# Expert gates added into a cleared DRAM array by 4-byte indirect DMAs in place of one-hot products

## The chip, the cores and the metric

The kernel runs on one core of a Trainium2 chip. The metric is the device time of one execution in microseconds (us); the median of three runs of the kernel before is 4406.32 us. A core has TensorE (PE in the rows, its weight loads PEld), VectorE (DVE), ScalarE (ACT), GpSimd (POOL) and SyncE (SP). SP and POOL issue DMAs, which run on 16 DMA engines.

## The reference

One inference step of a two-layer hybrid model over two streams: 128 prompt tokens and 512 sample tokens, 1024 channels each. Layer 0 mixes tokens by retention and a short convolution, layer 1 by gated DeltaNet and a long convolution. After each mixer comes a channel mixer (PEER): each token picks 16 of 16,384 experts for each of 8 heads. The part that the change touches:

```python
def peer_ffn(h, wq, keys, u_tab, v_tab):
    ...
    s1, i1 = lax.top_k(s[:, :, 0], TOPK)
    s2, i2 = lax.top_k(s[:, :, 1], TOPK)
    cand_s = (s1[..., :, None] + s2[..., None, :]).reshape(T, H_P, TOPK * TOPK)
    cand_i = (i1[..., :, None] * N_KEYS + i2[..., None, :]).reshape(T, H_P, TOPK * TOPK)
    top_s, sel = lax.top_k(cand_s, TOPK)
    eidx = jnp.take_along_axis(cand_i, sel, axis=-1)
    gates = jax.nn.softmax(top_s.astype(jnp.float32), axis=-1).astype(h.dtype)
    ...
        act = jax.nn.gelu(jnp.einsum('td,tkd->tk', xt, u_tab[et]))
        return jnp.einsum('tk,tkd->td', gt * act, v_tab[et])
```

So the result for a token is the sum over its 128 chosen experts (i1, i2) of gate x gelu(u . h) x v. A head chooses an expert at most once, but two heads may choose the same one; their gates then add up.

## The kernel before

**Streams and tiles.** The sample stream has four tiles of 128 tokens. Its first three go through the dense way: activations of all 16,384 experts on TensorE, weighted by a gate matrix that is zero where an expert isn't chosen. The fourth tile (`gt`), and the prompt's one tile, go the sparse way (`peer_gather`): for each of 128 places a row of u, later a row of v, is fetched for each token by an indirect DMA from POOL (`row<-u,eid`, `row<-v,eid`), and VectorE multiplies or adds (`gacc`).

**Stages of `peer_dense`,** once per layer.
- Acts stage. `acts` takes a block of 128 experts (one i1) at a time: load `ur`, split it into two parts `uh` and `ul` (`u_split`; the subtraction for `ul` goes to VectorE and POOL in turn), 24 products into `A`, gelu, store to DRAM (`wd`). It runs in the background, at a rate of blocks per us of foreground (RA, RG, RH, RM). The foreground makes, in order, the lists of experts (`peer_topk`, one tile after the other, with eight multiplications `eq` on POOL each), the gate matrix (`gate_matrix`), and, in layer 0 alone, the prompt's mixer of layer 1 (`mid`).
- `gate_matrix`. For each token two one-hot rows are made on VectorE or ScalarE (`o1`, with the gate in place of the one, and `o2`), a product `G` puts the gates of a token at (i2, i1), ScalarE evicts four tokens at a time into `gst`, and SP stores 1 MB at a time to DRAM (`gd<-gst`).
- Dense stage. For each block of 128 experts `load` brings `vr`, the activations and, for eight blocks at a time, the gates (`gt<-gd`); `stage` splits v (`vh`, `vl`, on VectorE for even blocks and POOL for odd ones), multiplies the activations by the gates (`w<-w,gt`) and splits the product (`wh`, `wl`); 18 products go into six accumulators (`dacc`). Some blocks of layer 1 are "fused": their activations are computed here and not in the acts stage. F1 sets how many (62 of 128 in effect).

In both stages a few steps of the last tile's `peer_gather` go in with each block (rates G0, G1, SP, SF).

**Order of work.** In the acts stage POOL keeps the order of the program; the other engines, and SP throughout, are ordered by the scheduler that builds the kernel. In the dense stage POOL, VectorE and ScalarE keep the program's order.

**The start.** `modulation` makes the 48 columns of scale and shift of layer 0 from 512 KB pieces (`w<-ada_c`, `w<-ada_k`) that SP loads; the first norm of layer 0 needs the first 16 of them.

## Time and profile before

| | |
|---|---|
| runs | 4391.36, 4406.32, 4421.05 us; median 4406.32 |
| profiled execution | span 4406.5 us (first to last instruction) |
| PE, DVE, POOL, ACT busy | 88%, 83%, 55%, 34% of the span |
| mean granted TensorE clock | 0.938 of full speed |
| DMA | 1158.45 MB, 263 GB/s over the span |

Layer 0's acts stage runs from about 780 to 1740 us (lists until 1098, gate matrix until 1409, then the prompt's mixer), its dense stage to 2340. Layer 1's acts stage runs from 3142 to 3580 (lists until 3372, then the gate matrix), its dense stage to 4390. Busy time of engines that work at the same time doesn't add up; what matters in a stage is which engine or transfer the others wait for.

### The profile page before, as it was taken

How to read it: one execution, taken by the hardware profiler on the slowest of the kernel's cores; microseconds unless marked ns; L12 is line 12 of the kernel's file. 1: busy time of each engine (PE TensorE's matmuls, PEld its weight loads, DVE VectorE, ACT ScalarE, POOL GpSimd, SP SyncE). 2: the span in 40 equal slices, each digit the busy share in tenths (PEclk: the TensorE clock that was granted, in tenths of full speed). 3: DMA queues.
4: the chain of work that ended last, by engine and by line, in shares of the span. 5: the costliest groups of instructions: out<-in, count | busy, mean ns of one | idle time of the engine just before them, and what ended most of it. 6: DMA issues, size and time to landing. Idle time of an engine off the chain costs nothing.

```text
span 4406.5 us, 56677 instructions
## 1 busy us (share of the span) xinstructions
PE 3868.7 (88%) x19422; PEld 3206.9 (73%) x19422; DVE 3677.7 (83%) x6843; ACT 1498.3 (34%) x2828; POOL 2411.8 (55%) x1520
## 2 busy tenths in 40 slices
PE   6797858899999998899998987887589989999997
PEld 4453547899998987677775456756579978888886
DVE  6568889998998656988887997659989978888888
ACT  2110131122774442233332253532224743333333
POOL 0126673686143754766655777425265247776664
PEclk9998878789999999999999989899899999999999
DMA  7548886886688788899987967237256699989994
GB/s 284 172 157 328 288 305 232 310 316 228 237 301 304 246 284 307 269 320 319 320 304 278 339 225 236 65 120 253 72 202 224 256 321 327 326 311 319 322 318 171
DMA packets 437040, 1158.45 MB, mean 263 GB/s; under 512 B 39440, under 2 KB 188048, under 8 KB 430352
## 3 DMA queue, kind: packets, MB, share of 16 engines
q1 hardware_dynamic: 282064, 591.69, 38.5%
q0 software_dynamic: 154688, 563.15, 36.3%
q8 instruction: 152, 2.49, 0.2%
q14 instruction: 136, 1.11, 0.1%
HBM read 1060.71 MB, written 93.98 MB: 262 GB/s over the span
## 4 chain that ended last, share of the span: by engine, by line
PE 31%; DVE 16%; issue 10%; POOL 3%; ACT 2%; DMA 2%; SPq 0%; DVEq 0%; POOLq 0%; ACTq 0%
PE dacc L161 14%; PE A L161 10%; DVE row L1227 3%; DVE gacc L1237 3%; POOL row L1203 2%; PE po L161 2%; PE G L161 1%; DVE wl L1308 1%; ACT wh L1307 1%; DMA row<-v,eid 1%; DMA row<-u,eid 1%; PE pt L161 1%; DVE ul L1308 1%; DVE eq L1179 1%; DVE o L1299 1%
## 5 line engine op out<-in xcount | busy, mean ns | idle before, releaser
L161 PE MATMUL A<-hHL,uh 128*128 128x384 f32 x4096 | 1110.4, 351 | 25.9 <-ACT uh L1307 25.7
L1203 POOL DMA_INDIRECT row<-v,eid x512 | 672.9, 1314 | 491.3 <-DVE gacc L1237 195.7
L1227 DVE SCALAR_TENSOR_TENSOR row<-row,hn 128x1024 f32<-128x1024 f32 x512 | 701.3, 1385 | 153.5 <-DMA row<-u,eid 151.8
L1203 POOL DMA_INDIRECT row<-u,eid x512 | 688.0, 1344 | 249.9 <-DVE row L1227 110.3
L161 PEld LDWEIGHTS A<-hHL,uh 128*128 128x128 f32 x4096 | 767.9, 196 | 40.0 <-ACT uh L1307 28.4
L1237 DVE SCALAR_TENSOR_TENSOR gacc<-row,gel,gacc 128x1024 f32<-128x1024 f32 x508 | 744.6, 1466 | 55.3 <-DMA row<-v,eid 50.6
L161 PE MATMUL A<-hHL,ul 128*128 128x384 f32 x2048 | 721.0, 353 | 65.4 <-DVE ul L1308 59.8
L1308 POOL TENSOR_TENSOR ul<-ur,uh 128x1024 fp32r<-128x1024 f32 x128 | 334.1, 2610 | 504.0 <-ACT uh L1307 456.0
L161 PE MATMUL dacc<-vh,wh 128*128 128x512 f32 x1536 | 458.7, 397 | 77.2 <-ACT wh L1307 77.1
L1308 POOL TENSOR_TENSOR vl<-vr,vh 128x1024 fp32r<-128x1024 f32 x128 | 355.3, 2776 | 267.9 <-ACT vh L1307 146.3
L161 PE MATMUL dacc<-vl,wh 128*128 128x512 f32 x1536 | 474.9, 392 | 1.3 <-POOL vl L1308 1.3
L161 PE MATMUL dacc<-vh,wl 128*128 128x512 f32 x1536 | 457.9, 390 | 7.9 <-DVE wl L1308 7.9
L1307 ACT CAST wh<-w 128x384 fp32r<-128x384 f32 (+1 forms) x226 | 133.0, 589 | 963.6 <-DVE w L1451 422.0
L161 PEld LDWEIGHTS A<-hHL,ul 128*128 128x128 f32 x2048 | 400.8, 196 | 79.1 <-DVE ul L1308 67.2
L161 PE MATMUL pt<-hT,w 128*128 128x128 f32 (+1 forms) x1664 | 395.6, 395 | 22.9 <-DMA w<-wq 11.6
L1307 ACT CAST uh<-ur 128x1024 fp32r<-128x1024 f32 x256 | 267.7, 1046 | 422.5 <-PE A L161 288.6
L161 PEld LDWEIGHTS dacc<-vh,wh 128*128 128x128 f32 x1536 | 282.1, 189 | 161.2 <-ACT wh L1307 110.6
L161 PEld LDWEIGHTS pt<-hT,w 128*128 128x128 f32 x1664 | 246.4, 199 | 164.6 <-issue 143.8
L161 PEld LDWEIGHTS dacc<-vh,wl 128*128 128x128 f32 x1536 | 287.7, 188 | 73.3 <-DVE wl L1308 11.4
L161 PEld LDWEIGHTS dacc<-vl,wh 128*128 128x128 f32 x1536 | 288.4, 188 | 60.4 <-POOL vl L1308 2.6
L1307 ACT CAST vh<-vr 128x1024 fp32r<-128x1024 f32 x256 | 267.2, 1044 | 4.5 <-DMA vr<-v 4.4
L1451 DVE TENSOR_TENSOR w<-w,gt 128x384 f32<-128x384 f32 x194 | 243.8, 1257 | 3.7 <-DMA w<-wd 3.7
(373 smaller groups left out, 6160.3 us busy)
## 6 DMA issues: line engine op xcount, KB each, us to landing
ur<-ut SPq DMA_DIRECT2D x256, 512.0 KB, 4.6
vr<-v SPq DMA_DIRECT2D x256, 512.0 KB, 6.7
gd<-gst SPq DMA_DIRECT2D x48, 1024.0 KB, 5.7
gt<-gd SPq DMA_DIRECT2D x96, 512.0 KB, 7.8
wd<-w SPq DMA_DIRECT2D x194, 192.0 KB, 3.8
w<-wd SPq DMA_DIRECT2D x194, 192.0 KB, 6.4
w<-ada_k SPq DMA_DIRECT2D x56, 512.0 KB, 6.4
w<-wq SPq DMA_DIRECT2D x48, 512.0 KB, 5.3
```

The source lines that it names most:

```text
L161: self.nc.tensor.matmul(out, lhsT, rhs, start=start, stop=stop)
L1179: V.tensor_tensor(eq, sf[:, h, :].unsqueeze(2).to_broadcast([P, TOPK, NSLOT]), self.iota50.unsqueeze(1).to_broadcast([P, TOPK, NSLOT]), op ...
L1203: self.nc.gpsimd.indirect_dma_start(out=t, out_offset=None, in_=table, in_offset=bass.IndirectOffsetOnAxis(ap=idx, axis=0))
L1227: V.scalar_tensor_tensor(u, u, 1.0, hn, op0=OP.mult, op1=OP.mult, accum_out=act[:, k:k + 1])
L1237: V.scalar_tensor_tensor(gacc, v, t[:, k:k + 1], gacc, op0=OP.mult, op1=OP.add)
L1299: V.tensor_scalar(o1, self.iota128, cols[:, 0, t:t + 1], cols[:, 2, t:t + 1], op0=OP.is_equal, op1=OP.mult)
L1307: self.nc.scalar.copy(hi, src)
L1308: (eng or self.nc.vector).tensor_tensor(lo, src, hi.bitcast(F32), op=OP.subtract)
L1451: V.tensor_tensor(w.rearrange("p (b t) -> p b t", t=TB), w.rearrange("p (b t) -> p b t", t=TB), g[:, :, e % GQ, :], op=OP.mult)
```

## The change

Six DRAM arrays, one per layer and dense tile, 8 MB each, are cleared by 24 DMAs from a tile of zeros (`clear`). When a tile's list is there, `scatter` adds its gates into its array: one indirect DMA per column of the list, 128 tokens x 4 bytes, with an addition at the destination. Of each tile, the 16 columns of one head go out without waits between them; the next 16 wait until those have landed, as two heads may meet at one place. When two additions of the same tile follow each other, a small memset of `tick0` stands between them. The address, expert x 128 + token, comes out of `peer_topk`. The loads of the gates wait for the last 16 additions of their tile.

Along with it: the last tile's list is made last, not first; all `ul` splits of the acts stage go to VectorE; the background's additions go in at 4.5 or 5 per block; 39 blocks of layer 1 are fused in place of 62; the gates are loaded for four blocks at a time; and rates change.

```diff
-TB = 16
-GQ = 8
+GQ = 4
+GS0 = 4.5
+GS1 = 5
+ZW = 256
+ZN = 4
...
-GE = 56
+GE = 80
...
-RM = 0.7
+RM = 0.9
...
-F1 = 64
+F1 = 40
...
-P1 = 1.35
+P1 = 1.4
...
+    def clear(self, l, n):
+        nc = self.nc
+        self.gd[l] = [self.tc.dram_tile([P * P * P, 1], F32, name=self.nm("gd")) for _ in range(n)]
+        self.filled[l] = []
+        src = self.zero.unsqueeze(1).to_broadcast([P, P * P // ZW // ZN, ZW])
+        for g in self.gd[l]:
+            parts = g.rearrange("(p z a w) o -> z p a (w o)", p=P, z=ZN, w=ZW)
+            self.filled[l].append([])
+            for z in range(ZN):
+                self.filled[l][-1].append(nc.sync.dma_start(parts[z], src))
+                yield
...
+    def scatter(self, st, l, tiles):
+        nc = self.nc
+        at = {n: 0 for n in range(len(tiles))}
+        before, now = dict(enumerate(self.filled[l])), {n: [] for n in at}
+        last, turn = None, 0
+        while at:
+            ready = [n for n in at if tiles[n] in st.gate]
+            if not ready:
+                yield
+                continue
+            turn += 1
+            n = ready[turn % len(ready)]
+            if n == last:
+                nc.gpsimd.memset(self.tick0, 0.0)
+            last, c, it = n, at[n], tiles[n]
+            i = nc.gpsimd.indirect_dma_start(
+                out=self.gd[l][n], out_offset=bass.IndirectOffsetOnAxis(ap=st.eid[it][:, c:c + 1], axis=0),
+                in_=st.gate[it][:, c:c + 1], in_offset=None, compute_op=OP.add)
...
+            self.after(i, before[n])
+            now[n].append(i)
+            at[n] += 1
+            if at[n] % TOPK == 0:
+                before[n], now[n] = now[n], []
+            if at[n] == P:
+                del at[n]
+            yield
+        self.filled[l] = [before[n] for n in range(len(tiles))]
...
-            un = self.u_split(i + 1, ur.pop(i + 1), up) if i + 1 < len(es) else None
+            un = self.u_split(0, ur.pop(i + 1), up) if i + 1 < len(es) else None
...
+            put += (GS0, GS1)[l] if st.gate else 0
+            while put >= 1:
+                put -= 1
+                next(places, None)
...
+                    self.after(nc.sync.dma_start(gg[g][:, n], gd[n][:, g * GQ:(g + 1) * GQ, :]), self.filled[l][n])
...
+                for it in tiles:
+                    self.peer_topk(st, it, True)
                 self.peer_topk(st, gt)
-                for it in tiles:
-                    self.peer_topk(st, it)
...
-            with self.tc.tile_pool(name=self.nm("gp"), bufs=2, reuse_waits="tile") as self.gp:
-                self.gate_matrix(st, tiles, gd)
...
+            self.finish_bg()
+            for _ in places:
+                pass
             lp = self.tc.alloc_tile_pool(name=self.nm("loads"), bufs=1, side="right", reuse_waits="tile")
             for e in range(LA):
                 load(e)
-            self.finish_bg()
...
+                fill = K.clear(0, ss.nt - 1)
+
                 def ahead():
                     for _ in islice(even_s, 23):
                         for _ in range(2):
                             next(K.modgen, None)
+                        next(fill, None)
                         yield
...
+                fill = K.clear(1, ss.nt - 1)
...
+                K.finish_bg()
+                for _ in fill:
+                    pass
```

The generators `clear` are advanced beside the mixers of layer 0 (`ahead`) and layer 1, but SP's queue is the scheduler's. On SP near the start, ahead of and behind the loads of x, before (w are the modulation's pieces):

```order
L350 DMA w_204<-ada_c 128x1024
L345 DMA w_209<-ada_k 128x1024
L1532 DMA x_s_47_318<-x_s 128x1024
...
L1532 DMA x_s_50_324<-x_s 128x1024
L350 DMA w_219<-ada_c 128x1024
L345 DMA w_224<-ada_k 128x1024
```

and now (gd are the six arrays, three per layer):

```order
L351 DMA w_212<-ada_k 128x1024
L1553 DMA x_s_47_321<-x_s 128x1024
...
L1553 DMA x_s_50_327<-x_s 128x1024
L395 DMA gd_620<-zero 128x16x256 x4
L395 DMA gd_621<-zero 128x16x256 x4
L395 DMA gd_622<-zero 128x16x256 x4
L395 DMA gd_17105<-zero 128x16x256 x3
L395 DMA gd_17106<-zero 128x16x256
L395 DMA gd_17105<-zero 128x16x256
L395 DMA gd_17106<-zero 128x16x256
L356 DMA w_222<-ada_c 128x1024
L395 DMA gd_17106<-zero 128x16x256 x2
```

Of the 24 clears 18 now stand between the fourth and the fifth modulation piece, four behind the fifth and two behind the seventh.

On POOL in layer 1's acts stage, in the list of the second tile, before:

```order
L1181 TENSOR_TENSOR eq_23934<-eq_23934,ci_23781 128x800
L1308 TENSOR_TENSOR ul_23941<-ur_23897,uh_23940 128x1024
L1181 TENSOR_TENSOR eq_23972<-eq_23972,ci_23781 128x800
L1203 DMA row_24010<-u,eid_23767 128x1024
L1181 TENSOR_TENSOR eq_24013<-eq_24013,ci_23781 128x800
L1308 TENSOR_TENSOR ul_24020<-ur_23976,uh_24019 128x1024
```

and now (gate and eid are the first tile's gates and addresses):

```order
L1240 TENSOR_TENSOR eq_22797<-eq_22797,ci_22594 128x800
L419 MEMSET tick_106 128x1
L421 DMA gd_17105<-gate_22588,eid_22580 2097152x1
...
L419 MEMSET tick_106 128x1
L421 DMA gd_17105<-gate_22588,eid_22580 2097152x1
L1240 TENSOR_TENSOR eq_22845<-eq_22845,ci_22594 128x800
```

Between two multiplications stood a split or a gather; now five additions stand there, each behind a memset (ten additions between every third pair). Counted over the queue: in layer 0, 139 additions, 56 memsets and some 20 gathers stand between the first gates and the last `eq`, then 245 additions, 97 gathers, 25 memsets and 14 multiplications by masks of the prompt's mixer (`off`) up to the dense stage's first split; in layer 1, 155 and 53, then 229 additions, 36 gathers and 27 memsets. VectorE has 52 `ul` splits of layer 0 and 63 of layer 1 ahead of the last list's reduction.

On VectorE at the end of layer 0's dense stage, before (dacc are the accumulators, w<-w,gt and wl the last expert's):

```order
L1451 TENSOR_TENSOR w_17861<-w_17861,gt_17487 128x384
L1308 TENSOR_TENSOR wl_17980<-w_17861,wh_17979 128x384
L1259 TENSOR_TENSOR dacc_13642<-dacc_13642,vr_18020 128x512
L1259 TENSOR_TENSOR dacc_13643<-dacc_13643,vr_18020 128x512
L1260 TENSOR_TENSOR x_s_47_318<-x_s_47_318,dacc_13642 128x512
```

and now:

```order
L1472 TENSOR_TENSOR w_16544<-w_16544,gt_16336 128x384
L1327 TENSOR_TENSOR wl_16675<-w_16544,wh_16674 128x384
L1299 SCALAR_TENSOR_TENSOR gacc_13574<-row_16546,gel_13571,gacc_13574 128x1024
...
L1299 SCALAR_TENSOR_TENSOR gacc_13574<-row_16636,gel_13571,gacc_13574 128x1024
L1321 TENSOR_TENSOR dacc_12255<-dacc_12255,vr_16819 128x512
L1321 TENSOR_TENSOR dacc_12256<-dacc_12256,vr_16819 128x512
L1299 SCALAR_TENSOR_TENSOR gacc_13574<-row_16666,gel_13571,gacc_13574 128x1024
```

The last tile's value rows (`gacc`), of which none stood behind the last expert's split, now have 38 there in layer 0, and 18 in layer 1.

## Rows read from the trace of the kernel before

**Rows 1.** Windows: busy us of each engine (instructions), granted clock, DMA share, GB/s.
```profile
780.00:1098.00 318.00, 290.91 (x1645) 287.61 (x1646) 287.50 (x556) 71.46 (x96) 225.52 (x128) 0.83 0.79 282
1098.00:1409.00 311.00, 295.17 (x2052) 285.74 (x2050) 295.69 (x730) 194.92 (x436) 102.03 (x62) 1.00 0.78 284
...
3142.00:3372.00 230.00, 190.77 (x1002) 185.40 (x1003) 205.21 (x400) 70.52 (x94) 158.42 (x79) 0.92 0.55 187
3372.00:3580.00 208.00, 187.06 (x1334) 182.94 (x1333) 188.29 (x447) 145.00 (x336) 49.79 (x29) 0.98 0.71 258
```

The columns after the window and its length are PE, PEld, DVE, ACT, POOL.

**Rows 2.** Chain of waits in layer 0's acts stage: start, us, what.
```profile
1648.69 4.16 PE A L161 x24
```

**Rows 3.** Windows of the products into A alone, on PE: busy us (count).
```profile
1098.00:1409.00 311.00, 183.66 (x907) 1.00 0.78 284
1409.00:1740.00 331.00, 224.97 (x1152) 0.96 0.79 274
3142.00:3372.00 230.00, 190.77 (x1002) 0.92 0.55 187
3372.00:3580.00 208.00, 116.98 (x557) 0.98 0.71 258
```

**Rows 4.** POOL's instructions in order of time: start, us, [idle before <-releaser].
```profile
324.59 0.94 POOL L1203 DMA_INDIRECT row<-u,eid  x1 [0.30 <-issue]
329.68 1.44 POOL L1203 DMA_INDIRECT row<-u,eid  x1 [0.31 <-issue]
...
1100.34 0.95 POOL L1203 DMA_INDIRECT row<-u,eid  x1 [0.16 <-issue]
```

**Rows 5.** Groups by line on POOL: busy us, mean ns of one, then idle before.
```profile
L1181 POOL TENSOR_TENSOR eq<-eq,ci 128x800 f32<-128x800 f32 x80 | 166.3, 2081 | 119.4 <-DVE eq L1179 103.0 <-DVE eid L1187 11.8 <-DVE ci L1164 3.5
L935 POOL TENSOR_TENSOR off<-e,msk 128x512 f32<-128x512 f32 x70 | 102.7, 1484 | 34.3 <-PE bY L161 12.3 <-DVE hc L869 10.5 <-DVE e L928 6.3
...
L226 POOL DMA_DIRECT2D w<-ev_t x16 | 8.7, 547 | 108.7 <-PE pt L161 102.2 <-PE pn L161 5.7 <-POOLq L1723 0.8
```

**Rows 6.** Windows of the row gathers alone, on POOL: busy us (count).
```profile
892.00:1098.00 206.00, 59.35 (x41) 0.87 0.77 273
...
1409.00:1740.00 331.00, 93.08 (x73) 0.96 0.79 274
3196.00:3372.00 176.00, 35.62 (x25) 0.92 0.61 208
```

**Rows 7.** VectorE in order of time: the end of the first list, each layer.
```profile
892.39 0.22 DVE L1187 CAST eid<-ef 128x128 int32<-128x128 f32 x1
...
3196.29 0.22 DVE L1187 CAST eid<-ef 128x128 int32<-128x128 f32 x1
```

**Rows 8.** PE in order of time: the first expert product of each layer.
```profile
1740.16 1.22 PE L161 MATMUL dacc<-vh,wh 128*128 128x512 f32 x2 [10.13 <-ACT wh L1307]
...
3580.25 1.22 PE L161 MATMUL dacc<-vh,wh 128*128 128x512 f32 x2 [12.17 <-ACT wh L1307]
```

**Rows 9.** DMA issues: count, median us from issue to landing.
```profile
row<-u,eid POOLq DMA_INDIRECT x512, 6.8
```

**Rows 10.** Windows at the start, all engines; the last column is GB/s.
```profile
0.00:100.00 100.00, 59.94 (x252) 48.61 (x252) 60.00 (x146) 21.99 (x47) 8.39 (x19) 0.98 0.83 298
20.00:30.00 10.00, 7.36 (x35) 7.37 (x36) 7.79 (x27) 4.23 (x12) 0.00 (x0) 1.00 1.03 415
```

**Rows 11.** Chain of waits in the dense stages: layer 0, then layer 1.
```profile
1855.43 4.39 PE dacc L161 x18
...
1864.51 4.41 PE dacc L161 x18
...
3752.77 5.45 PE dacc L161 x24
...
3765.16 5.45 PE dacc L161 x24
```

**Rows 12.** Groups by line on VectorE: the value rows.
```profile
L1237 DVE SCALAR_TENSOR_TENSOR gacc<-row,gel,gacc 128x1024 f32<-128x1024 f32 x508 | 744.6, 1466 | 55.3 <-DMA row<-v,eid 50.6
```

More of the change, by code (lines that the diff above doesn't have):

```diff
@@ L316, in setup @@
         gdn_g = sw[:, o:o + 1]; o += 1
+        self.pidx = sw[:, o:o + 1]; o += 1
+        self.zero = cp.tile([P, ZW], F32, name="zero")
+        nc.vector.memset(self.zero, 0.0)
+        self.tick0 = cp.tile([P, 1], F32, name="tick0")
+        self.gd, self.filled = {}, {}
         half = cp.tile([P, 140], F32, name="halved")
@@ L376, in load_c_rows, with after @@
             nc.vector.scalar_tensor_tensor(c, th, 1.0, c, op0=OP.add, op1=OP.mult)
+    def clear(self, l, n):
[9 more added lines that the diff above has]
+                yield
+    def after(self, ins, others):
+        dep = mybir.DependencyInfo(mybir.DependencyClass.Sync, mybir.DependencyReason.DATA)
+        for o in others:
+            self.tc.add_manual_dep(ins.ins, o.ins.name, dep, reason="gates")
+    def scatter(self, st, l, tiles):
[16 more added lines that the diff above has]
+                in_=st.gate[it][:, c:c + 1], in_offset=None, compute_op=OP.add)
+            key = f"gates{l}_{n}_{c // TOPK}"
+            self.tc.declare_no_dep(i.ins, group=key, reason="other experts of the same tokens")
+            self.tc.add_to_no_dep_group(key, i.ins)
+            self.after(i, before[n])
[7 more added lines that the diff above has]
+        self.filled[l] = [before[n] for n in range(len(tiles))]
     def normed(self, st):
@@ L1361, in peer_dense @@
         N = len(tiles) * P
-        NTB = N // TB
-        gd = self.tc.dram_tile([NTB, P, P, TB], F32, name=self.nm("gd"))
+        gd = [g.rearrange("(i p t) o -> p i (t o)", i=P, p=P) for g in self.gd[l]]
         wd = self.tc.dram_tile([P, P, N], F32, name=self.nm("wd"))
@@ L1378, in load @@
             nc.sync.dma_start(vr, A[f"v{l}"][e * P:(e + 1) * P, :])
-            for n in range(0, NTB, 8):
-                if e == 0 or e % GQ == 4 + n // 8 and e + GQ < P:
+            for n in range(len(tiles)):
+                if e == 0 or e % GQ == 1 + n and e + GQ < P:
                     g = e // GQ + (e > 0)
                     if n == 0:
-                        gg[g] = ld("gt", [P, NTB, GQ, TB], bufs=2)
-                    nc.sync.dma_start(gg[g][:, n:n + 8],
-                                      gd[n:n + 8, :, g * GQ:(g + 1) * GQ, :].rearrange("b p i t -> p b i t"))
+                        gg[g] = ld("gt", [P, len(tiles), GQ, P], bufs=3)
+                    self.after(nc.sync.dma_start(gg[g][:, n], gd[n][:, g * GQ:(g + 1) * GQ, :]), self.filled[l][n])
             if e in fused:
@@ L1396, in peer_dense @@
         steps = self.peer_gather(st, gt, l, st.hn)
+        places = self.scatter(st, l, tiles)
         with self.banks(5), self.tc.tile_pool(name=self.nm("up"), bufs=2, reuse_waits="tile") as up:
-            self.behind(self.acts(st, l, [e for e in range(P) if e not in fused], up, wd, steps), RA)
+            self.behind(self.acts(st, l, [e for e in range(P) if e not in fused], up, wd, steps, places), RA)
             with self.topk_space():
@@ L1598, in build, with rows @@
                 K.dgp = tc.alloc_tile_pool(name="dg", bufs=DG, side="right", reuse_waits="tile")
-                K.behind(K.laned(K.peer_rows(sp, 0, 1), lane="p"), RS)
+                fill = K.clear(1, ss.nt - 1)
+                def rows():
+                    for k, _ in enumerate(K.laned(K.peer_rows(sp, 0, 1), lane="p")):
+                        if k % 10 == 9:
+                            next(fill, None)
+                        yield
+                K.behind(rows(), RS)
                 K.odd_mixer(ss, phs)
                 K.dgp.release()
+                K.finish_bg()
+                for _ in fill:
+                    pass
         with K.banks(), K.base(NB2):
```

58 lines of the change are left out of this document (9 added, 49 removed).

## The prediction

> **What bounds the kernel now.** The busy shares of the whole span (the table above) hide the two stretches that the change rebuilds, so the first view is the windows in which the gate matrix is made [rows 1]: 311 us in layer 0, 208 us in layer 1. PE and VectorE are both busy nearly throughout, POOL for 102 and 50 us: that pair sets the pace, and POOL looks free. Next, what a block of 128 experts costs PE: 24 products, 4.16 us [rows 2]. The count of those products by window [rows 3], over 24, says how far the blocks are: in layer 0 38 beside the gate matrix, 48 beside the prompt's mixer, and so 42 of the 128 before, while the top-k lists are made (780 to 1098); in layer 1 42 and 23. In the gate stretches a block took 311/38 = 8.2 and 208/23 = 9.0 us instead of 4.16; that is what can be won. Last come POOL's own rows [rows 4 to 6], since the change takes the work to that queue.
>
> **1. The one-hot products go.** 384 products, 384 VectorE operations and as many of ScalarE or fewer leave each layer. If only PE counted, layer 0 would need, after the lists, 76 blocks (the new order has 52 of 128 done by then) x 4.16 = 316 us, and for the prompt's mixer beside them 331 - 48 x 4.16 = 131 us [rows 3]: 447 us. In layer 1 the stage gets 89 blocks instead of 66; 63 stand ahead of the last list operation, 26 behind: 108 us.
>
> **2. The additions come to POOL.** 384 per layer, of 128 elements each. None is in this trace. Nearest is the row gather, also indirect, also 128 rows from POOL. Where two follow each other and VectorE is idle it holds POOL for 0.94 us, with a gap of 0.30 us; beside a busy VectorE it takes 1.44 us; the shortest gap, behind another kind of instruction, is 0.16 us [rows 4]. So a slot of POOL is 0.94 + 0.16 = 1.10 us at least and 1.44 + 0.31 = 1.75 us at most by these rows. I take **1.25 us**, the two rows back to back: VectorE has less to do than before, and 4 bytes take as many addresses as 4 KB. An addition is also a read before the write; no row prices that.
>
> On POOL's queue the additions stand, four or five behind each block, ahead of the list multiplications (eq) of the next tiles and of the gathers. VectorE waits for eq in its own order, and behind that wait are the splits that PE needs, all of them VectorE's now. So the list stage walks at POOL's pace.
>
> Layer 0, from the first gates at 892 [rows 7]: 139 additions up to the last eq (174 us), 24 eq at 2.08 (50) [rows 5], 20 gathers at 1.45 + 0.16 (32) [rows 6], 56 small clearing instructions at a gap of 0.16 (9), and three waits of a lone tile for its own last 16 additions at 6 us (18; a gather lands after 6.8 us [rows 9]): 283 us, to 1175; before, the lists were through by 1098. Then 245 additions (306), 97 gathers at 1.27 + 0.16 (139) [rows 6], the mixer's masks (24) [rows 5], 4 for clearing: 473 us, to 1648. PE would be through at 1175 + 447 = 1622, so POOL is last; with 3 us for a split the first expert product comes at 1651 instead of 1740 [rows 8]: **-89 us**.
>
> Layer 1, from 3196 [rows 7]: 155 additions (194), 50 for eq, 9 and 18: 271, to 3467. Then 229 additions (286), 36 gathers at 1.42 + 0.16 (57), 4, and 15 of waits: 362, to 3829. PE's 26 blocks are through at 3575, so it idles some 250 us. The last addition lands 6.8 us later, and from there to the first product I take the 12.2 us that PE idled before it until now [rows 8]: 3848 instead of 3580, **+268 us**.
>
> With 1.10 us a slot, layer 0 gives 1154 and then PE's 447: -136; layer 1 +211. With 1.75: +103 and +460.
>
> **3. The clears.** 24 DMAs of 2 MB, 50.3 MB. In the code they stand beside two mixers, but SP's queue has all 24, layer 1's too, right behind the loads of x, 18 of them ahead of the fifth modulation weight, and all of layer 0 waits for the modulation. DMA moved 298 GB/s in the first 100 us and 415 GB/s in its best 10 us there [rows 10]: 169 or 121 us for 50.3 MB. I take **+145 us**, the middle: DMA is 0.83 busy in that stretch, so there is little idle time for them to fill. That the 48 stores of the gate matrix go is worth nothing by itself: POOL or PE ends those stages.
>
> **4. Fused blocks.** Layer 1's dense stage computes 39 blocks of activations itself instead of 62. Two experts of which one is fused take 12.39 us there; two of layer 0, none fused, 9.08 [rows 11]. 23 x 3.31 = **-76 us**. The 23 blocks go to the acts stage, where by step 2 PE has the time.
>
> **5. The last tile's gathers come later.** Its list is now the last, and its rates are lower: 38 of its 128 value rows in layer 0, 18 in layer 1, stand behind the last expert's split on VectorE, where none did. 38 x 1.47 [rows 12] = 56 us, some 11 beside the last two experts' products: **+45 us** ahead of the next layer's norm; 18 x 1.47 = 26, less 9: **+17 us** at the end.
>
> **The sum.** -89 + 45 + 268 - 76 + 17 + 145 = +310 us on the profiled execution's span of 4406.5 us, which is the median of the runs (4406.32): **4717 us**. With 1.10 us a slot and 121 us of clears: -136 + 45 + 211 - 76 + 17 + 121 = +182, 4588 us. With 1.75 and 169: 103 + 45 + 460 - 76 + 17 + 169 = +718, 5124 us.
>
> **Two rules beside the rows.** The rows show 0.94 us of POOL for 128 rows while VectorE is idle [rows 4]. The Trainium skill ("DMA: Bandwidth & Descriptors", section "Anatomy of one DMA") calls descriptor generation small: many can be emitted before the extra cost shows, and most of a DMA's fixed 2 us is the receipt of its write. By that rule an addition would hold POOL for next to nothing, the first rival below; the gathers disagree. The same rows rise to 1.44 us beside VectorE's work. "SBUF — State Buffer" of the Trainium skill (its box on VectorE blocking DMAs issued from GpSimd) says that GpSimd can't write descriptors while VectorE is in certain modes; the rows agree in direction, and by it the sum moves towards 5124.
>
> **Rivals.**
> - Additions nearly free on POOL (a slot of 0.3 us, the bare gap). Then PE bounds both acts stages: in layer 0 10 more blocks in the list stage, 42 us less the 27 that PE was idle there (318 - 291 [rows 1]), then 447 and 3: 1098 + 15 + 450 = 1563, -177; in layer 1 21 more, 87 less 39 [rows 1], then 108 and 19: 3547, -33. -177 + 45 - 33 - 76 + 17 + 145 = -79: **4328 us, faster**. It decides below a slot of about 0.5 us. For it: POOL is idle more than half of both stretches. Against: the rows of 0.94 us.
> - Additions priced like POOL's direct DMA, 0.547 us [rows 5] + 0.16: layer 0 by PE, -177; layer 1 by POOL, 3641, +61; -177 + 45 + 61 - 76 + 17 + 145 = +15, **4422 us, the same**. Against: that DMA reads no index.
> - The clears run where the code has them and cost nothing: 4717 - 145 = **4572 us**. Against: the order on SP.
> - An addition costs more than a gather, being read, added and written: at 1.75 us **5124 us**. For it: the 16 DMA engines are 0.55 to 0.79 busy in those windows [rows 1], and 49,152 tiny writes a layer join them.
>
> **How the numbers follow.** Chances: the forecast (slots of 1.0 to 1.6 us, clears at the start) 0.62; heavy additions 0.15; clears spread 0.08; priced like direct DMAs 0.08; nearly free 0.07. The likeliest gives 4717 us. The range goes from 4410, which takes in the direct price, to 5000 (about 1.6 us a slot); it leaves out the free additions and the heavy ones, some 2 in 10. The runs before lie between 4391 and 4421 us, so about 1%, 44 us, is what a measurement can tell from no change. Faster by more: 0.07; within: 0.08; slower: 0.85.
>
> **What would show it.** Clears: SP issues 24 DMAs out of the zero tile from about 22 us, DMA stays full to about 170 us, and PE's first projections come some 145 us later. Slots: the POOL rows gd<-gate, their mean and gap; POOL nearly full from the first gates to the first expert product in both layers, and PE's busy share and granted clock in layer 1's acts stage far below the 187 of 208 us and 0.98 of [rows 1]. Fused: a dense stage of layer 1 shorter by about 60 us. Tail: 38 gacc rows after layer 0's last expert product. I am wrong if a slot is below 0.7 us, or if the modulation weights don't wait for the clears.

## Result, and the profile after

The changed kernel takes 5371.38 us (median of 4 runs, 5354.68 to 5380.69) against 4410.58 us of the kernel before beside it: 1.2185 times as long, 95% interval 1.2144 to 1.2227. The direction was forecast, the size was not: 4717 us and a range up to 5000. The profiled execution has a span of 5378.8 us, against 4406.5.

The page of the changed kernel in 40 slices, tenths busy, shows the two acts stages at a glance (slices 8 to 15 and 27 to 33, counted from 0, of 134 us each):

```profile
PE   0579777886767777899949978488676301999896
...
POOL 0014573688888883666656783416888888666665
PEclk9999688777888889999979988798888655999998
```

POOL stands at 8 in nearly all of them. In layer 1's, PE goes down to 0 with the granted clock at half speed, on an engine that before was busy for 187 of 208 us there [rows 1]. The windows by stage (PE, PEld, DVE, ACT, POOL, clock, DMA share, GB/s), first the start, then each layer's lists and the rest of its acts stage:

```profile
0.00:100.00 100.00, 8.59 (x40) 8.50 (x40) 17.97 (x67) 15.18 (x32) 2.02 (x7) 1.00 0.99 342
100.00:200.00 100.00, 19.76 (x90) 19.42 (x90) 15.61 (x25) 0.00 (x0) 0.00 (x0) 1.00 0.97 327
...
1044.50:1413.50 369.00, 273.38 (x1388) 265.21 (x1388) 141.88 (x242) 66.40 (x92) 313.55 (x235) 0.77 0.59 144
1413.50:2152.70 739.20, 528.99 (x2945) 499.50 (x2945) 311.35 (x762) 187.83 (x342) 562.56 (x383) 0.86 0.68 182
3688.40:4057.80 369.40, 257.89 (x1272) 250.84 (x1272) 123.52 (x237) 80.83 (x111) 314.43 (x235) 0.85 0.52 114
4057.80:4557.20 499.40, 125.08 (x625) 121.59 (x623) 69.04 (x91) 38.19 (x55) 416.29 (x292) 0.63 0.45 80
```

POOL is busy for 0.76 to 0.85 of the four later windows. In three of them the 0.3 us ahead of each of its DMAs make up most of the rest; in the second, which ends layer 0's stage, such gaps are 93 of the 177 us left, 30 are waits of its gathers for other engines, and the last 49 lie behind its last gather. PE in order of time gives the edges: the end of the clears, the first expert product of each layer (answers to [rows 8]), and two waits, of which the first was 10 us before and the second is new:

```profile
169.05 2.29 PE L353 MATMUL mod<-c_cols,w 128*128 128x2 f32 x10 [137.59 <-DMA w<-ada_k]
...
2152.68 1.22 PE L162 MATMUL dacc<-vh,wh 128*128 128x512 f32 x2 [10.12 <-ACT wh L1326]
...
2820.23 2.15 PE L470 MATMUL xT<-cst,xn 128*128 128x128 f32 x9 [69.99 <-DVE xn L460]
...
3485.83 1.51 PE L470 MATMUL xT<-cst,xn 128*128 128x128 f32 x6 [67.47 <-DVE xn L460]
...
4557.19 1.22 PE L162 MATMUL dacc<-vh,wh 128*128 128x512 f32 x2 [319.23 <-ACT wh L1326]
```

The lists end on VectorE at these times (the first lists' addresses come at 1044.54 and 3688.42):

```profile
1413.50 0.23 DVE L1249 CAST eid<-ef 128x128 int32<-128x128 f32 x1
...
4057.84 0.23 DVE L1249 CAST eid<-ef 128x128 int32<-128x128 f32 x1
```

From these edges the 972 us between the two spans are, stretch by stretch:

| stretch | before | after | difference |
|---|---|---|---|
| start to layer 0's first gates | 892.4 | 1044.5 | +152 |
| layer 0, first gates to first expert product | 847.8 | 1108.1 | +260 |
| layer 0, dense | 600.0 | 597.2 | -3 |
| layer 0's last product to layer 1's first gates | 856.1 | 938.5 | +82 |
| layer 1, first gates to first expert product | 384.0 | 868.8 | +485 |
| layer 1, dense | 803.3 | 779.4 | -24 |
| after the last product | 22.9 | 42.3 | +19 |

Three quarters stand in the two acts stages. POOL in order of time shows a slot (from the start of one DMA on POOL to the start of the next), first where VectorE is idle, then in a list with one tile ready, where a clearing instruction (the memset of `tick0`) follows each addition (answers to [rows 4]), and last the end of POOL's queue in layer 0's stage, its last addition and its last gather:

```profile
4308.09 1.56 POOL L421 DMA_INDIRECT gd<-gate,eid  x1 [0.30 <-issue]
4309.95 1.56 POOL L421 DMA_INDIRECT gd<-gate,eid  x1 [0.31 <-issue]
...
1060.12 1.58 POOL L421 DMA_INDIRECT gd<-gate,eid  x1 [0.19 <-issue]
1061.14 0.67 POOL L419 MEMSET tick<- 128x1 f32 x1
1062.01 1.57 POOL L421 DMA_INDIRECT gd<-gate,eid  x1 [0.19 <-issue]
...
1996.16 2.59 POOL L421 DMA_INDIRECT gd<-gate,eid  x1 [0.19 <-issue]
...
2102.71 0.94 POOL L1265 DMA_INDIRECT row<-u,eid  x1 [0.31 <-issue]
```

An addition holds POOL for 1.56 us and starts 1.87 us after the one ahead of it; the row gather, back to back, held it for 0.94 with the same gap of 0.30. The clearing instruction costs nothing: the trace has it start inside the addition's 1.58 us, and the next addition starts 1.89 us after the one before, as without it. Groups by line on POOL in the four windows of the acts stages, in their order:

```profile
L421 POOL DMA_INDIRECT gd<-gate,eid x140 | 246.4, 1760 | 49.1 <-issue 37.8 <-DMA gd<-gate,eid 9.6 <-DVE eq L1238 0.6
...
L421 POOL DMA_INDIRECT gd<-gate,eid x245 | 426.4, 1740 | 76.9 <-issue 72.1 <-DMA gd<-gate,eid 4.8
L1265 POOL DMA_INDIRECT row<-u,eid x97 | 113.5, 1170 | 50.8 <-issue 21.0 <-DVE row L1289 13.1 <-DVE bc_d L275 6.4
...
L421 POOL DMA_INDIRECT gd<-gate,eid x156 | 268.7, 1723 | 56.0 <-issue 52.7 <-DVE eid L1247 1.6 <-DMA gd<-gate,eid 1.4
...
L421 POOL DMA_INDIRECT gd<-gate,eid x229 | 377.3, 1648 | 69.1 <-issue 67.4 <-DMA gd<-gate,eid 1.4 <-DMA row<-u,eid 0.3
```

With the idle time ahead of them, the additions took 295, 503, 325 and 446 us (246.4 + 49.1 and so on), 2.11, 2.05, 2.08 and 1.95 us each, above the 1.87 us back to back where VectorE is idle. (The windows share an addition at their edges, so the counts add up to 770 and not 768.) The waits for landed additions, which the groups of 16 make, are 9.6, 4.8, 1.4 and 1.4 us: next to nothing.

In layer 1 POOL's last addition ends at 4550.2 us, 7 us before the first expert product. In layer 0 the last one ends at 1998.7 us, 154 us before it. In between PE is busy for 117 us, with nine more blocks, the end of the prompt's mixer and its list; POOL has 49 gathers and four masks left, and waits some 29 us for other engines between them. What the additions did to that end is to hold it up: the mixer's 14 masks (`off`), which stand between them on POOL's queue, come from 1840 to 2014 us and not from 1442 to 1521 as before (1487 to 1559 in the run without additions below).

### The profile page after: what moved, and what is told of

Read it like the earlier page. It is cut to its first block, busy times and chain, and to the rows that moved or that the text cites. A ratio compares the mean times of both kernels' runs of the same rounds, so it can differ in the third digit from the quotient of the medians.

```text
span 5378.8 us, 53190 instructions
## 1 busy us (share of the span) xinstructions
PE 3861.1 (72%) x17868; PEld 3152.5 (59%) x17868; DVE 3305.9 (61%) x6133; ACT 1280.9 (24%) x2253; POOL 3393.7 (63%) x2341
## 5 line engine op out<-in xcount | busy, mean ns | idle before, releaser
L421 POOL DMA_INDIRECT gd<-gate,eid x768 | 1315.7, 1713 | 250.7 <-issue 229.7
L162 PE MATMUL A<-hHL,uh 128*128 128x384 f32 x4096 | 1169.0, 369 | 40.1 <-ACT uh L1326 38.9
L1289 DVE SCALAR_TENSOR_TENSOR row<-row,hn 128x1024 f32<-128x1024 f32 x512 | 639.8, 1264 | 730.0 <-DMA row<-u,eid 717.8
L162 PE MATMUL A<-hHL,ul 128*128 128x384 f32 x2048 | 767.5, 375 | 430.9 <-DVE ul L1327 430.6
L162 PEld LDWEIGHTS A<-hHL,uh 128*128 128x128 f32 x4096 | 839.0, 212 | 50.0 <-ACT uh L1326 41.2
L1265 POOL DMA_INDIRECT row<-u,eid x512 | 655.4, 1280 | 333.9 <-DVE row L1289 183.0
L1299 DVE SCALAR_TENSOR_TENSOR gacc<-row,gel,gacc 128x1024 f32<-128x1024 f32 x508 | 698.6, 1375 | 127.1 <-DMA row<-v,eid 121.3
L162 PEld LDWEIGHTS A<-hHL,ul 128*128 128x128 f32 x2048 | 433.6, 212 | 464.3 <-DVE ul L1327 461.6
L1327 DVE TENSOR_TENSOR ul<-ur,uh 128x1024 fp32r<-128x1024 f32 x233 | 288.2, 1247 | 101.3 <-ACT uh L1326 79.2
L1472 DVE TENSOR_TENSOR w<-w,gt 128x384 f32<-128x384 f32 x217 | 282.7, 1303 | 52.7 <-DMA gt<-gd 52.7
```

What stands on the lines that cost most here:

```text
L162: self.nc.tensor.matmul(out, lhsT, rhs, start=start, stop=stop)
L421: i = nc.gpsimd.indirect_dma_start(out=self.gd[l][n], out_offset=bass.IndirectOffsetOnAxis(ap=st.eid[it][:, c:c + 1], axis=0), in_=st.gate ...
L1265: self.nc.gpsimd.indirect_dma_start(out=t, out_offset=None, in_=table, in_offset=bass.IndirectOffsetOnAxis(ap=idx, axis=0))
L1289: V.scalar_tensor_tensor(u, u, 1.0, hn, op0=OP.mult, op1=OP.mult, accum_out=act[:, k:k + 1])
L1299: V.scalar_tensor_tensor(gacc, v, t[:, k:k + 1], gacc, op0=OP.mult, op1=OP.add)
L1327: (eng or self.nc.vector).tensor_tensor(lo, src, hi.bitcast(F32), op=OP.subtract)
```

## Experiments

**The price of an addition by itself.** Two kernels issue only indirect DMAs from POOL, 48 of each 4-byte kind in a row. The core of the first:

```diff
+        for c in range(N):      # gathered
+            G.indirect_dma_start(out=e4[:, c:c + 1], out_offset=None, in_=U, in_offset=off(far, c))
...
+        for c in range(N):      # written; then the same with OP.add
+            put("wr", c, vals[:, c:c + 1], off(far, c), None)
...
+        for c in range(N):      # on 32 partitions
+            put("part", c, vals[:32, c:c + 1], off(far, c, 32), OP.add)
...
+        for _ in range(96):
+            V.tensor_tensor(b0, b0, b1, op=OP.mult)
+        for c in range(N):
+            put("busy", c, vals[:, c:c + 1], off(far, c), OP.add)
```

Expected:

> Leaves out the whole model; only POOL's indirect DMAs run, in a row, 48 of each 4-byte kind and 12 of each 4 KB kind. Theory 1 (an accumulating scatter costs POOL more by itself): gathers of 4 KB and 4 B at 0.94 us with a gap of 0.30, plain 4-byte writes at the same, additions at 1.56 us whether the places are neighbours or far apart and whether they are 4 B or 4 KB; 32 partitions a good deal less if it is paid per row written, the same if it is paid per instruction; beside a busy VectorE more. Theory 2 (the DMA engines hold POOL back because 4-byte read-and-writes in memory are slow): the first additions of a row take 0.94 us and later ones more, far-apart places more than neighbours, 4 KB rows most. Theory 3 (scatters are dear, added or not): plain writes cost 1.56 us too.

Groups by line of this kernel (busy us, mean ns, idle before; near: neighbouring places, far: 64 KB apart; wide: 4 KB rows):

```profile
L70 POOL DMA_INDIRECT g_busy<-vals,far x48 | 106.7, 2222 | 14.5 <-issue 14.5
L70 POOL DMA_INDIRECT g_ad<-vals,near x48 | 74.1, 1545 | 75.1 <-DMA g_ad<-vals,near 72.8 <-issue 2.3
L70 POOL DMA_INDIRECT g_far<-vals,far x48 | 74.1, 1544 | 19.2 <-issue 12.2 <-DMA g_ad<-vals,near 7.0
L70 POOL DMA_INDIRECT g_part<-vals,far x48 | 63.6, 1326 | 14.5 <-issue 14.5
L70 POOL DMA_INDIRECT g_wr<-vals,far x48 | 46.0, 959 | 14.5 <-issue 14.5
L82 POOL DMA_INDIRECT e<-u,far x48 | 45.3, 944 | 25.4 <-DMA row<-u,near 13.2 <-issue 12.2
L70 POOL DMA_INDIRECT g_wide<-row,near x12 | 18.5, 1545 | 3.5 <-issue 3.5
```

Theory 1 holds. A scatter that only writes costs what a gather costs (0.96 and 0.94 us), so theory 3 falls. An addition costs 0.59 us more, the same for neighbours, far places and 4 KB rows, and the same while the clears of this kernel kept the DMA engines full (those of the near places): then POOL waits between them for landings, but the addition itself isn't longer. So theory 2 falls too. On 32 partitions it still takes 1.33 us, so it is paid per instruction rather than per place. The second kernel asks how that goes on, and what a busy VectorE adds by kind of operation:

```diff
+        for n, key in ((16, "a16"), (64, "a64"), (128, "a128")):
+            for c in range(N):
+                put(key, c, vals[:n, c:c + 1], off(far, c, n), OP.add)
...
+            put("w32", c, vals[:32, c:c + 1], off(far, c, 32), None)
...
+        for key, f in (("tt", lambda: V.tensor_tensor(b0, b0, b1, op=OP.mult)),
+                       ("ts", lambda: V.tensor_scalar(b0, b1, 1.0, None, op0=OP.mult)),
+                       ("stt", lambda: V.scalar_tensor_tensor(b0, b0, 1.0, b1, op0=OP.mult, op1=OP.mult))):
```

Expected:

> Leaves out the whole model. Additions on 16, 64 and 128 partitions, plain writes and 4-byte gathers on 32, additions with a clearing instruction behind each, and additions beside a VectorE that runs two-input (tensor_tensor), one-input (tensor_scalar) and scalar-and-two-input operations. If the additions' extra 0.6 us is paid per instruction: 16 partitions still take 1.25 to 1.3 us (a straight line through the 1.33 us of 32 and the 1.54 us of 128 gives 1.29 and 1.40 for 16 and 64), and writes and gathers of 32 take 0.70 to 0.95 us. If it is paid per index: 16 partitions take under 1.0 us. A clearing instruction behind an addition takes 0.6 to 0.7 us each time, a slot of addition and clearing 2.3 to 2.5 us. Beside VectorE: if POOL's writes of DMA descriptors wait for VectorE's hold on a shared port, two-input operations cost additions most (2.2 us), one-input operations less or more but not nothing; if any busy VectorE does the same, all three 2.2 us.

POOL in order of time in this kernel: additions on 16, 64 and 128 partitions, then 128 beside tensor_tensor and beside tensor_scalar.

```profile
110.70 1.29 POOL L66 DMA_INDIRECT g_a<-vals,far  x1 [0.30 <-issue]
...
195.07 1.41 POOL L66 DMA_INDIRECT g_a<-vals,far  x1 [0.30 <-issue]
...
284.71 1.55 POOL L66 DMA_INDIRECT g_a<-vals,far  x1 [0.30 <-issue]
...
562.31 2.22 POOL L66 DMA_INDIRECT g_tt<-vals,far  x1 [0.30 <-issue]
...
660.85 1.88 POOL L66 DMA_INDIRECT g_ts<-vals,far  x1 [0.30 <-issue]
```

and its groups of plain writes and gathers on 32 partitions:

```profile
L80 POOL DMA_INDIRECT e<-u,far x48 | 41.9, 872 | 14.5 <-issue 14.5
L66 POOL DMA_INDIRECT g_w<-vals,far x48 | 41.8, 871 | 14.5 <-issue 14.5
```

The price is mostly one per instruction: an eighth of the places takes 0.83 of the time (1.29 of 1.55 us), and of the 0.59 us that an addition costs beyond a write, 0.46 are there on 32 partitions (1.33 less 0.87). Beside VectorE an addition goes to 1.88 us (one-input operations) or 2.22 (two-input ones). The first clearing instructions behind additions again lay inside the addition's span, for a slot of 1.9 us; most later ones there waited 0.99 us each for something that the trace doesn't name, for a slot of 2.80 us; the changed kernel's rows above don't show that, and its reason stays open.

**Writes in place of additions, in the kernel.**

```diff
-                in_=st.gate[it][:, c:c + 1], in_offset=None, compute_op=OP.add)
+                in_=st.gate[it][:, c:c + 1], in_offset=None)
```

> The changed kernel with 4-byte indirect writes in place of additions; leaves out that the gates of two heads which chose the same expert add up. Theory 1 (the addition itself holds POOL 0.6 us longer than a gather): a slot falls from 1.87 to about 1.25 us, layer 0's stretch from the first gates to the first expert product from 1108 to about 880 us, layer 1's from 869 to about 630, the whole to 4850 to 4950 us. Theory 3 (a scatter costs POOL that much with or without addition): slots stay at 1.8 to 1.9 us and the whole within 1% of 5371.

Measured: 4990.63 us, 1.1347 times the kernel before (1.1302 to 1.1392), 381 us below the changed kernel. A slot of POOL, and layer 1's first expert product:

```profile
4051.18 0.96 POOL L421 DMA_INDIRECT gd<-gate,eid  x1 [0.30 <-issue]
...
4156.18 1.22 PE L162 MATMUL dacc<-vh,wh 128*128 128x512 f32 x2 [170.11 <-ACT wh L1326]
```

Slots of 1.27 us back to back; over the four windows of the acts stages a write with the idle time ahead of it took 1.51, 1.43, 1.51 and 1.36 us, 0.57 to 0.62 less than an addition. Layer 1's stage takes 675 us (from 3481.1) and layer 0's 931 (1019.4 to 1950.5). 768 additions x 0.6 us are 461; the two stages are 371 us shorter. Layer 1's stage is within 4% of the forecast 652 us (3848 - 3196), in part by luck, as the slots are longer than 1.25 us and the waits shorter than forecast. Layer 0's, forecast at 759, is 172 us longer: here too the last write ends (at 1797.2 us) 153 us before the first product, so the price of a slot isn't all that the prediction missed there.

**No additions at all.** The call, its group and its waits are left out of `scatter`.

> The changed kernel without any of the 768 additions, their waits and their clearing instructions; leaves out the gates of three tiles (the dense stage multiplies by zeros), all else as changed. If POOL's additions are all that is dear in the acts stages: layer 0 from the first gates to the first expert product about 671 us (the prediction's terms for a stage that PE bounds), layer 1 about 351 us, a dense stage of 779 us, and with the clears (+152) and the leftover gathers (+67) ahead of it the whole 4380 to 4450 us. If other parts of the change (all ul splits on VectorE, the order of lists, the rates) cost as well: layer 0 over 750 or layer 1 over 420 us, the whole above 4500 us.

Measured: 4516.45 us, 1.0256 times before (1.0224 to 1.0288); so the additions cost 855 of the 961 us. First expert products, layer 0 and layer 1:

```profile
1778.19 1.22 PE L162 MATMUL dacc<-vh,wh 128*128 128x512 f32 x2 [10.13 <-ACT wh L1314]
...
3685.12 1.22 PE L162 MATMUL dacc<-vh,wh 128*128 128x512 f32 x2 [3.83 <-ACT wh L1314]
```

Layer 0's stage is 759 us (from 1018.7), layer 1's 389 (from 3296.4), its lists through 135 and 104 us after the first one instead of 369 and 369. So the additions on POOL's queue were what the lists waited for. But both stages are longer than a PE-bound stage was thought to be (671 and 351): when the lists get shorter, fewer blocks stand beside them and more behind (101 of layer 0 instead of 76: 2426 products into A, 1828 in the changed kernel, over 24). Free additions, too, would have made this kernel slower than before, and not the 4328 us of the first rival.

**Clears held beside the mixers.**

```diff
-        self.nc.tensor.matmul(out, lhsT, rhs, start=start, stop=stop)
+        self.late = self.nc.tensor.matmul(out, lhsT, rhs, start=start, stop=stop)
...
                 self.filled[l][-1].append(nc.sync.dma_start(parts[z], src))
+                self.after(self.filled[l][-1][-1], [self.late])
```

> The changed kernel with each clear waiting for the matrix product that stands ahead of it in the program, so that the clears run beside the mixers and not ahead of the modulation weights. If the 152 us of later start are the clears and the mixers have room for them: first gates of layer 0 at 890 to 910 instead of 1044 us, whole 5200 to 5260 us. If the 50 MB are paid wherever they run (transfers late for the mixers): whole 5320 to 5380 us.

Measured: 5288.96 us, 82 less. The clears now run from 115 to 3048 us, and the first 100 us have PE busy for 59 us again, as in [rows 10]:

```profile
0.00:100.00 100.00, 59.22 (x256) 47.84 (x256) 62.19 (x152) 22.79 (x49) 8.37 (x19) 1.00 0.87 301
```

Layer 0's first gates come at 927.8 us: of the 152 us, 117 are back, and 35 stay, with layer 0's 25 MB beside the mixer; layer 1's cost nothing there (936 us from the last product to the next first gates, 938 in the changed kernel). 117 less 10 that layer 0's stage grows are the 107 us between the two profiled spans; the medians differ by 82, and the time lies between the two expectations. Single profiles are only so sharp: PE's first projections come at 200.8 to 203.9 us in all six profiled kernels that have the clears at the start, but layer 0's first gates between 1018.7 and 1045.7, though nothing that was edited stands ahead of them. So less than some 27 us at that edge is not read as an effect here.

**The prompt's leftover gathers back in the acts stage.**

```diff
                 K.odd_mixer(ss, phs)
                 K.dgp.release()
-                K.finish_bg()
```

> The changed kernel without the line that finishes the prompt's gathers ahead of layer 1's split of the hidden state; they go into the acts stage as before. If PE's idle time there (67 us) is just lost by that line: 67 us less, 5290 to 5320 us. If POOL is the bound of the acts stage from the first gates on: the some 53 gathers (1.1 us and a gap of 0.3 each, 74 us) take their time back from POOL as far as they fall behind the first gates: 5320 to 5380 us.

Measured: 5346.15 us, 25 less (interval of the ratio 1.2097 to 1.2182, against 1.2144 to 1.2227: it overlaps). PE's wait of 67 us is 14, and layer 1's first gates come 25 us sooner after layer 0's last product (913 us). In the stretch ahead of layer 1's first gates VectorE is now busy for 156 of 160 us, with lists, splits and 21 value rows:

```profile
3500.00:3660.00 160.00, 116.62 (x558) 100.43 (x557) 155.53 (x700) 41.76 (x58) 48.29 (x28) 0.88 0.39 128
```

The stage behind the first gates keeps its 868 us, so POOL there took nothing back. Of the 67 us no more than 25 show in the time, and those aren't clear of noise; that VectorE took back the rest, ahead of the first gates, fits this row but is not shown.

**No fused blocks in layer 1.**

```diff
-F1 = 40
+F1 = 0
```

> The changed kernel with F1 = 0: all 128 blocks of layer 1 have their activations made in the acts stage, where PE is idle for 319 us behind the lists. If POOL bounds that stage: its length stays (869 us from the first gates to the first expert product, within 20), PE's gap shrinks by about 39 x 4.16 = 162 us, and the dense stage is 39 x 3.31 = 129 us shorter: whole 5230 to 5260 us. If the splits and products of 39 more blocks hold the additions up: whole 5290 to 5370 us.

Measured: 5265.62 us, 106 less. Layer 1's stage grows by 22 us to 891, PE's gap falls to 53 us, and the dense stage takes 672.8 us, 107 less. Per block 2.7 us, not 3.31. (Of the 118 us between the two profiles, 85 lie in layer 1; the others lie ahead of it, where nothing changed.) What PE waits for in layer 1's dense stage behind its first product, first in the changed kernel, then here:

```profile
PE dacc L162 <- ACT wh L1326: 33.8, 38, 2.3
PE dacc L162 <- DVE wl L1327: 20.0, 10, 2.0
```

```profile
PE dacc L162 <- ACT wh L1326: 96.6, 83, 37.2
```

PE's busy time in the stage falls from 724 to 561 us, 4.17 us a block, but its idle time doubles, from 56 to 112 us. One wait of 37.2 us, for the second expert, is most of that: VectorE, which keeps the program's order, has 28 rows of the last tile to multiply ahead of that expert's product with the gates. The other 82 of these waits sum to 59 us, near the 54 of the changed kernel.

**The three together** (clears held, gathers back, F1 = 0):

> The changed kernel with the clears held beside the mixers, the prompt's leftover gathers back in the acts stage, and F1 = 0. If the three act on stages of their own, their gains add: 82 + 25 + 120 to 140 us, 5125 to 5150 us, still 16% above the kernel before, because none of them takes an addition off POOL. If they overlap (transfers of the clears delay what the others free): 5170 to 5250 us.

Measured: 5163.84 us, 1.1716 times before: 208 less, where the parts sum to 213. They add, within the spread, and none touches the main cost.

**Additions only once the lists are made.**

```diff
-            put += (GS0, GS1)[l] if st.gate else 0
+            put += (GS0, GS1)[l] if len(st.gate) == st.nt else 0
```

> The changed kernel with additions only once all four lists are made. If the additions ahead of the lists' multiplications on POOL's queue are the cost (lists through 369 us after the first one instead of 135 without additions): both layers' stages become some 200 us shorter, whole about 4950 to 5000 us. If POOL's sum is the bound and the order isn't: the lists are through after 104 to 135 us, and 384 additions of 1.87 us, with gathers and masks, stand behind them; layer 0's stage 135 + 718 + 164 + 33 = 1050 instead of 1108 us (the clearing instructions of a lone tile and its waits go), layer 1's 104 + 718 + 50 + 19 = 891 instead of 869: whole 5300 to 5380 us.

Measured: 5454.2 us, 83 more. The lists are through after 135 and 106 us, as in the run without additions, and nothing is won. Layer 1's stage takes 898 us, as POOL's sum had it (891): there the order isn't the cost. Layer 0's takes 1203, not 1050. Its windows behind the lists:

```profile
1172.70:2107.20 934.50, 680.12 (x3708) 648.06 (x3706) 334.91 (x722) 226.99 (x396) 696.10 (x441) 0.85 0.63 159
2107.20:2241.30 134.10, 0.00 (x1) 0.00 (x0) 38.90 (x130) 3.66 (x6) 97.11 (x64) 0.50 0.37 73
```

and a group of POOL in the first of them, with its wait:

```profile
L977 POOL TENSOR_TENSOR X<-X,msk 128x512 f32<-128x512 f32 x2 | 2.6, 1290 | 106.9 <-ACT X L976 106.9
```

The 76 blocks behind the lists take 4.5 additions each, 342 of 384; the other 42 stand at the end, with PE idle. During the lists POOL is busy for 78 of 135 us, and behind them it stands for 107 us, 103 of them in one wait, before two steps of the prompt's mixer (`X`) that wait for ScalarE, with additions queued behind them; in the changed kernel these steps come up without a wait. So here the order does cost: POOL, which has the longest sum, is kept idle by what stands ahead of the additions. What a version without that wait takes was not run.

**One tile of three by additions.** The kernel before, with one tile's gates added into the layout of its gate matrix and the other two made by one-hot products. 128 additions per layer would lie in POOL's idle half. The blocks beside the gate matrix go in faster as well (RG 0.18 for 0.12, RH 0.4 for 0.27).

```diff
-                self.peer_topk(st, gt)
-                for it in tiles:
-                    self.peer_topk(st, it)
+                for it in ([0, gt] if ADDED[l] and True else [gt, 0]) + tiles[1:]:
+                    self.peer_topk(st, it, it == 0 and ADDED[l])
...
-                self.gate_matrix(st, tiles, gd)
+                self.gate_matrix(st, tiles[1:] if ADDED[l] else tiles, gd[P // TB:] if ADDED[l] else gd)
```

> The kernel before with one dense tile of three by additions (128 per layer, a quarter array of 8 MB per layer cleared beside the mixers) and two by one-hot products. If an addition costs only POOL time, and POOL had half of these stages idle: the gate matrix is a third shorter, by PE about 50 us in layer 0 and 37 in layer 1, some of it lost to clears: 4310 to 4360 us. If additions beside a saturated VectorE take 2.2 us and more and delay the splits and gathers on POOL's queue: PE waits for POOL, 4400 to 4500 us.

Measured: 4592.49 us, 1.0417 times before (1.0398 to 1.0437). Waits in layer 0's lists (engine, line, waited for, us, times, longest):

```profile
DVE ef L1237 <- POOL eq L1236: 34.5, 13, 5.8
PEld A L166 <- POOL ul L1372: 24.5, 8, 8.5
```

Before, VectorE waited 8.0 us for `eq` in the lists and PE's weight loads 0.5 us for POOL's splits; now these stand behind additions of 1.85 us on POOL's queue. Layer 0's stage is 63 us longer and layer 1's 97. The next version keeps the lists free of them: additions in layer 0 only, only once the lists are made, and the lists in the order of the kernel before (RH is 0.27 again, RG stays 0.18).

```diff
-GS0 = 1.4
+GS0 = 1.7
...
-ADDED = (True, True)
+ADDED = (True, False)
...
-            put += (GS0, GS1)[l] if st.gate else 0
+            put += (GS0, GS1)[l] if len(st.gate) == st.nt else 0
```

> The kernel before with one of three dense tiles by additions in layer 0 alone, and these only once the four lists are made; 4 clears (8 MB) beside the mixer. If the 186 us that one tile cost in both layers were the lists' and splits' wait behind additions on POOL's queue: the lists are through some 205 us after the first gates as before, the gate matrix is about 50 us shorter, the clears take 10 to 20 us: 4360 to 4400 us. If the ul splits on POOL, now behind additions of about 2 us and clearing instructions, hold PE in the gate stage and beside the mixer: 4410 to 4480 us.

Measured: 4488.37 us, 1.0179 times before (1.0153 to 1.0205). The lists are through 211 us after the first gates (935.0 to 1145.9), near the 205 of before, but the first gates come 43 us late, with the four clears ahead of them (that these are the cause isn't shown), and the rest of the stage takes 688 us instead of 643. PE's longest kind of wait in that rest (1098 to 1840):

```profile
PE A L166 <- POOL ul L1372: 23.0, 11, 5.5
```

POOL is busy for 0.83 to 0.89 of 1300 to 1700 us in this kernel: the splits, the gathers and 128 additions fill it. In the kernel before PE waited for no split on POOL in that stretch. No version of the experiments beats the kernel before.

## Why the prediction was wrong in size

**Where the miss lies.** The profile is 662 us above the forecast: 349 in layer 0's acts stage (+260 for -89), 217 in layer 1's (+485 for +268), 52 in the fused blocks, 37 ahead of layer 1's first gates, 7 in the clears, and next to nothing elsewhere.

**The step that failed is part 2's slot: "I take 1.25 us".** The counts were right: 139, 245, 155 and 229 additions forecast, 140, 245, 156 and 229 in the windows. Their time was 960 us by the forecast (174 + 306 + 194 + 286) and is 1570 (295 + 503 + 325 + 446), 610 us more. The run with plain writes splits this. Its writes took 1109 us in the same windows, so 461 of the 610 us are the addition: 0.6 us each, which the prediction named ("a read before the write; no row prices that") and then took at nothing. The other 149 us, 0.19 a slot, a plain write would have cost too: the prediction took the two rows back to back with VectorE idle, though in the same sum it priced its gathers at 1.27 to 1.45 us and a gap, their means beside VectorE [rows 6]. The upper bound failed likewise. Its 1.75 us came from one gather of 1.44 us beside VectorE; an addition beside VectorE takes up to 2.22 + 0.30, and the trace of the kernel before has longer gathers too:

```profile
1095.42 1.79 POOL L1203 DMA_INDIRECT row<-u,eid  x1
```

**The mechanism was right in the lists and in layer 1.** "The list stage walks at POOL's pace" holds: 369 us in both layers, 135 and 104 without additions. With 1.87 us for 1.25, the sums of part 2 for the lists give 139 x 0.62 = 86 and 155 x 0.62 = 96 us more, 283 + 86 = 369 and 271 + 96 = 367. That this meets the measured time so closely is in part luck: the additions took 2.11 and 2.08 us there, and the waits for landings (9.6 and 1.4 us for 18 each) and the clearing instructions (nothing for 9) less than forecast. PE's idle 250 us in layer 1 are 319, with POOL last. The heavy rival, at 5124, came nearest; it, too, was bounded by gathers.

**Layer 0's stage: "POOL is last", with 3 us for a split behind it, failed too.** POOL's queue ends 49 us before the first expert product, and its last 105 us, behind the last addition, have 37 us of idle time: the stage ends with the prompt's mixer and its list, on PE and VectorE. By POOL's time the stage has 111 us beyond 1.87 us a slot (283 + 86 and 473 + 152, less 848 with 3 for the split, is +149; measured +260). Of these some 45 are the 0.18 us by which the 245 additions there exceed 1.87, 25 the gathers (164 us instead of 139, of which 30 are waits for other engines), and 46 what lies behind the last gather, where 3 were taken; smaller terms give 5 back. With plain writes this end is as long, 153 us behind the last write, so a right price alone would not have given layer 0's time.

**Clears: right.** PE's first projections come at 202.8 us instead of 58.9, +144 for +145; the +152 at the first gates has some of the spread told above. DMA moved 342 and 327 GB/s, between the two bounds. They could have been hidden, as the rival had it, but for 35 us.

**Fused blocks: mis-sized**, -24 for -76. PE's busy time in the stage fell by 69 us (793 to 724), 3.0 a block, near the 3.31; but its idle time, which the prediction took as unchanged, grew by 45 us (11 to 56): PE waits for the splits of VectorE and ScalarE (54 us behind the first product, against 10 before). A price read where PE is last doesn't hold beyond the point where something else is.

**Tail of the gathers: right** at the end (+19 for +17); in layer 0 the wait ahead of the next norm is 70 us instead of 10, +60 for +45.

**One line was overlooked:** the gathers are finished ahead of layer 1's split, PE waits 67 us. The diff in the text has it; the prediction had no term for it. Its undoing gave 25 us, not clear of noise; with the 60 us of the tail that is about the +82 of this stretch.

**The rule weighed beside the rows** was that of the Trainium skill ("DMA: Bandwidth & Descriptors", "Anatomy of one DMA"), that descriptor generation is small. Here 16 places cost POOL 1.29 us and 128 cost 1.55: the part that grows with the places is small, as it says, but the instruction's own time isn't. The other rule of the Trainium skill ("SBUF — State Buffer", the box on VectorE blocking DMAs issued from GpSimd) agrees in part. It speaks of VectorE's two-port modes, which a copy in float32 enters. Here VectorE's work lengthens an addition, from 1.55 us to 1.88 and 2.22, but most beside two-input operations, and which modes these ran in no trace shows.

## What to carry to other kernels

An indirect DMA is an instruction of POOL with a time of its own (here 0.94 us for a gather or a write, 1.55 for an addition, 0.30 between), 4 B or 4 KB alike, so count instructions, not bytes, before moving work there; 384 of them a layer are 720 us of a queue that looked half idle in stages of 438 and 960. A price for an operation that the trace doesn't hold deserves a range as wide as what is unknown of it, and where a sum stands or falls with it, the worst plausible value is tried first. And an engine's idle half is no free room if others wait for its instructions one by one: a third of the additions still cost 4%, with splits and list steps waiting behind them.

## What the runs showed of the hardware that was not expected

- An accumulating scatter costs POOL 0.59 us more than a plain one (1.545 against 0.959 us on 128 partitions), the same for 4 bytes and 4 KB a row, near or far, and with the DMA engines full.
- It is mostly a price per instruction: an addition took 1.29 us on 16 partitions, 1.33 on 32, 1.41 on 64, 1.55 on 128.
- Beside VectorE it goes to 1.88 us (one-input operations) and 2.22 us (two-input ones) that took 0.69 and 1.22 us themselves.
- A small clearing instruction behind an addition starts within the addition's span (1061.14 inside 1060.12 to 1061.70) and takes no time of its own from the queue in the changed kernel; in the second small kernel most of them waited 0.99 us.
